# Decode logits of a hybrid decoder step: products on GpSimd, sums on VectorE

## The chip, the core and the metric

The kernel runs on one core of a Trainium2 chip. The metric is the device time of one execution in microseconds. Engines are named as in the profile: PE is TensorE, DVE is VectorE, ACT is ScalarE, POOL is GpSimd, SP is SyncE.

## What is computed

One step of a decoder with two parallel branches (attention and a gated short convolution), for a prompt of 512 rows plus 16 learned ones, and for 8 decode sequences of 4 new rows each with 512 past rows in a paged cache. All is float32; the model width is 2048, with 8 heads of 128 channels. Cut to what matters here:

```python
q, k, v, ga, cb, cc, ch, gc, ma, mc = split(rmsnorm(x) @ w_in)
z = einsum('bqhd,bkhd->bhqk', q, k) * HEAD_DIM ** -0.5 + b_sb      # the logits
log_keep = where(mask, log_sigmoid(-z), 0)
after = cumsum(log_keep, axis=3, reverse=True) - log_keep
attn = where(mask, exp(log_sigmoid(z) + after), 0)
a = einsum('bhqk,bkhd->bqhd', attn, v) * silu(ga)
c = cb * causal_conv(cc * ch) * silu(gc)
y = x + rmsnorm((sigmoid(ma + b) * (a @ w_pa) + sigmoid(mc + b2) * (c @ w_pc)) @ w_out)
```

The change concerns the logits `z` of the decode rows against their past: for each of the 8 sequences, 4 pages of 128 past keys, 8 heads and 4 query rows, a product over 128 channels.

## The kernel before

**Matrix products.** Weights are loaded by SP's queue in blocks of 1024 x 128 (`w_load`, L234, five buffers `raw`). `w_split` takes each apart: ACT casts the high part `whi` (L240), DVE subtracts it and writes the low part `wlo` (L241), in three buffers each. PE then makes three products per block and half of the rows (L256 plain, L944 in the scheme of seven products that the gate and output projections use, whose sums of weights DVE forms in L956 to L972). So every block that PE multiplies has first passed ACT and then DVE.

**Order of the stages.** First the norm of the rows and the first queries (to about 120 us); then the heads: `head_now` for four heads, with projections of k, v and q and the prompt's attention, whose masks POOL makes (L625), and `head_later` for four more; then the projections `pair` of the attention's gate, the convolution and the merge gates; then the rest of the attention, the two branch projections and the output.

**Decode attention** is a generator, `decode_steps`, which the other stages call for a step at a time (`dec_step`, `dec_group`), so that its instructions are written among theirs. A unit is a half of the heads and one sequence: 16 units of 4 pages. The first six units (`DEC1`) are called for by the heads, the other ten by the gate projections, one or two pages for each group of them. A unit loads its four query rows, broadcast to all 128 partitions, in two tiles `qb` of two rows and 4 heads x 128 channels (L745, POOL's queue, three buffers). Each page loads 128 keys, one to a partition, with 512 channels of four heads (`kpage`, L730, POOL's queue, three buffers). Then DVE works out 16 logits a key, each with one instruction (L754) that multiplies 128 channels of a key with those of a query, writes the products to a tile that nobody reads, and puts the sum into one column of `z_all`. After all pages the steps "logits", "weights" and "values" follow.

The order of the instructions within each engine is not the program's: a planner simulates the program on a timeline and writes each engine's order by it, except where `pin` (`keep_in_program_order`) ties an instruction to its place. `first` ties the loads of the first unit of each part. Once written, each engine's order is fixed and it works it off in order; semaphores hold an instruction until what it needs is done.

Of the kernel before, what the change touches and what calls it, by code (L numbers as in the profile page):

```python
# [9 lines left out]
F32 = mybir.dt.float32  # L10
# [3 lines left out]
ALU = mybir.AluOpType  # L14
# [3 lines left out]
P = 128  # L18
# [42 lines left out]
def hybrid_step_kernel(  # L61
# [7 lines left out]
    pe, act, dve, pool = nc.tensor, nc.scalar, nc.vector, nc.gpsimd  # L69
# [416 lines left out]
    z_all = dp.tile([P, NPG, DB, H, DT], F32, name="z_all")  # L486
# [239 lines left out]
    def page_load(t, cache, b, pg, cs):  # L726
        i = b * NPG + pg
        if i not in page_reg:
            page_reg[i] = pool.value_load(pt_i[0:1, i:i + 1], min_val=0, max_val=NPOOL - 1)
        return pool.dma_start(t, cache[bass.ds(page_reg[i], 1), :, cs].rearrange("o s c -> (o s) c"))  # L730

    def decode_steps():
# [2 lines left out]
        units = [(hf, b) for hf in range(2) for b in range(DB)]  # L735
        for said, part in (("part", units[:DEC1]), ("logits", units[DEC1:])):
            with tc.tile_pool(name="dec1", bufs=2, side="right") as d1:
                for hf, b in part:
                    cs = slice(hf * 512, (hf + 1) * 512)
                    qts = []  # L740
                    first = pin if (hf, b) in (units[0], units[DEC1]) else lambda x: x
                    for i in range(2):
                        qt = d1.tile([P, 2, 512], F32, name="qb", bufs=3)
                        r0 = b * DT + 2 * i
                        first(pool.dma_start(qt, q_scr[r0:r0 + 2, cs].unsqueeze(0).broadcast_to([P, 2, 512])))  # L745
                        qts.append(qt)
                    for pg in range(NPG):
                        kt = d1.tile([P, 512], F32, name="kpage", bufs=3)
                        first(page_load(kt, kc, b, pg, cs))
                        for i, qt in enumerate(qts):  # L750
                            for t in range(2):
                                for h in range(4):
                                    junk = d1.tile([P, P], F32, name="junk", bufs=2)
                                    dve.tensor_tensor_reduce(  # L754
                                        out=junk, in0=kt[:, h * P:(h + 1) * P], in1=qt[:, t, h * P:(h + 1) * P],
                                        scale=1.0, scalar=0.0, op0=ALU.mult, op1=ALU.add,
                                        accum_out=z_all[:, pg, b, 4 * hf + h, 2 * i + t:2 * i + t + 1])
                        yield
            yield said
        hl.append(hlctx.enter_context(tc.tile_pool(name="headin", bufs=1, side="right")))  # L760
        BHT = DB * H * DT
# [16 lines left out]
        with tc.tile_pool(name="dec2", bufs=1, side="right") as d2:  # L778
            def tl(name, n=1):
                return d2.tile([P, n * BHT], F32, name=name)  # L780

            e, l, r, t = tl("de", 4), tl("dl", 4), tl("dr", 4), tl("dt", 4)
# [39 lines left out]
        for g in range(2):  # L822
            for hf in range(2):
# [29 lines left out]
                for hh in range(4):  # L853
                    h = 4 * hf + hh
# [4 lines left out]
                yield  # L859

    dec = decode_steps()
    dec_at = set()

# [573 lines left out]
```

## Time and profile before

| | us |
|---|---|
| median of 3 runs | 1598.49 |
| lowest and highest | 1595.0 and 1600.42 |
| the profiled execution | 1598.94 |
| its span, first to last instruction | 1597.3 |
| granted TensorE clock in it | 0.993 of full speed |

The span is what the views of the trace cut up; times in them count from its start. A group's row reads: line, engine, operation, what it writes and reads, shapes, count, then the busy time, the mean nanoseconds of one, and the idle time of the engine just before them with what ended it. A row of a stretch reads: start and end, length, then for each engine the busy time and the number of its instructions, the granted clock, the share of DMA time and GB/s. A row of the timeline reads: start, duration, engine, line, operation, operands, count. The costliest groups by engine: PE's matmuls of L944 and L256, and on DVE the weight parts of L241 and the logits:

```profile
L241 DVE TENSOR_TENSOR wlo<-raw,whi 128x1024 fp32r<-128x1024 f32 x247 | 301.2, 1221 | 82.9 <-ACT whi L240 81.5
L754 DVE CUSTOM_DVE_ANT_0 junk<-kpage,qb 128x128 f32<-128x128 f32 x1024 | 245.1, 285 | 3.7 <-DMA qb<-q_scr 3.3
```

Consecutive instructions of DVE overlap in the records by some tens of nanoseconds, so a group's busy time can be more than it adds to the queue.

### The profile page before, as it was taken

The numbers are of one execution on the slowest core, as the hardware profiler recorded it, in microseconds if no ns is written. First come the engines' busy times: TensorE is split into PE (matmuls) and PEld (weight loads), VectorE is DVE, ScalarE is ACT, GpSimd is POOL, SyncE is SP. The second block draws the span as 40 slices with busy tenths as digits, with TensorE's granted clock in tenths as the row PEclk, the third lists the DMA queues.
The fourth block names the chain that finished last, engine by engine and source line by source line (L and its number), as shares of the span: only waits on it lengthen the run. The fifth ranks groups of instructions, "written<-read, shape, count | busy, mean of one in ns | idle before, by whom it ended". The sixth has DMA issues, their size and how long they took to land.

```text
span 1597.3 us, 32319 instructions
## 1 busy us (share of the span) xinstructions
PE 1567.6 (98%) x12172; PEld 1533.7 (96%) x12172; DVE 1268.8 (79%) x3574; ACT 752.7 (47%) x1339; POOL 234.6 (15%) x428
## 2 busy tenths in 40 slices
PE   9999999999999999999999999999899999999997
PEld 8999999999999999999999999999897789999997
DVE  6328999956799999999999996667666657877776
ACT  6335555435444444444454444446645543355562
POOL 1033333222111011010011100001203320000000
PEclk9999999999999999999999999999999999999999
DMA  8246556344555445355356554433868875433345
GB/s 247 81 137 180 169 164 187 110 127 138 167 162 146 139 140 150 117 152 159 107 180 187 161 155 130 125 121 115 279 186 265 253 240 179 152 101 99 100 137 187
DMA packets 300674, 252.77 MB, mean 158 GB/s; under 512 B 11521, under 2 KB 268613, under 8 KB 299701
## 3 DMA queue, kind: packets, MB, share of 16 engines
q1 hardware_dynamic: 272021, 160.45, 34.7%
q0 software_dynamic: 28368, 89.98, 17.0%
q8 instruction: 95, 1.56, 0.4%
q14 instruction: 62, 0.51, 0.1%
q10 hardware_dynamic: 128, 0.27, 0.1%
HBM read 217.95 MB, written 32.71 MB: 157 GB/s over the span
## 4 chain that ended last, share of the span: by engine, by line
PE 89%; DMA 4%; issue 2%; DVE 2%; ACT 1%; POOL 0%; DVEq 0%; POOLq 0%; SPq 0%; ACTq 0%
PE mm L944 32%; PE mm L256 24%; PE o L944 23%; DMA vpage<-in_cache_v 2%; PE mm L321 2%; PE z L321 1%; PE z L677 1%; PE o L687 1%; DMA raw<-in_w_in 1%; PE z L608 1%; PE z L1378 1%; DMA sg<-a_scr 1%; DMA gt<-gate_scr 1%; DVE wlo L241 1%; PE tp L829 0%
## 5 line engine op out<-in xcount | busy, mean ns | idle before, releaser
L240 ACT CAST whi<-raw 128x1024 fp32r<-128x1024 f32 x247 | 259.4, 1051 | 356.0 <-PE mm L944 122.3
L241 DVE TENSOR_TENSOR wlo<-raw,whi 128x1024 fp32r<-128x1024 f32 x247 | 301.2, 1221 | 82.9 <-ACT whi L240 81.5
L944 PE MATMUL mm<-h_hi,whi 128*128 128x272 f32 (+1 forms) x1152 | 332.6, 289 | 0.0
L944 PE MATMUL mm<-h_lo,whi 128*128 128x272 f32 (+1 forms) x1152 | 332.4, 289 | 0.0
L944 PE MATMUL mm<-h_hi,wlo 128*128 128x272 f32 (+1 forms) x1152 | 332.3, 290 | 0.0
L944 PE MATMUL o<-t_hi,whi 128*128 128x272 f32 (+1 forms) x864 | 250.0, 289 | 1.0 <-DVE c L970 1.0
L944 PE MATMUL o<-t_lo,whi 128*128 128x272 f32 (+1 forms) x864 | 250.2, 290 | 0.0
L944 PE MATMUL o<-t_hi,wlo 128*128 128x272 f32 (+1 forms) x864 | 249.8, 289 | 0.0
L754 DVE CUSTOM_DVE_ANT_0 junk<-kpage,qb 128x128 f32<-128x128 f32 x1024 | 245.1, 285 | 3.7 <-DMA qb<-q_scr 3.3
L944 PEld LDWEIGHTS mm<-h_hi,whi 128*128 128x128 f32 x1152 | 217.4, 189 | 0.0
L944 PEld LDWEIGHTS mm<-h_hi,wlo 128*128 128x128 f32 x1152 | 216.9, 189 | 0.1
L944 PEld LDWEIGHTS mm<-h_lo,whi 128*128 128x128 f32 x1152 | 216.8, 188 | 0.1
L241 DVE TENSOR_TENSOR wlo<-s,whi 128x1024 fp32r<-128x1024 f32 x126 | 154.0, 1222 | 63.9 <-ACT whi L240 62.5
L240 ACT CAST whi<-s 128x1024 fp32r<-128x1024 f32 x126 | 132.0, 1048 | 152.9 <-PE mm L944 52.8
L256 PE MATMUL mm<-h_lo,whi 128*128 128x280 f32 (+1 forms) x640 | 187.7, 293 | 0.0
L256 PE MATMUL mm<-h_hi,wlo 128*128 128x280 f32 (+1 forms) x640 | 187.1, 293 | 0.0
L256 PE MATMUL mm<-h_hi,whi 128*128 128x280 f32 (+1 forms) x640 | 186.7, 292 | 0.0
L944 PEld LDWEIGHTS o<-t_hi,whi 128*128 128x128 f32 x864 | 162.9, 189 | 1.5 <-DVE c L970 1.5
L944 PEld LDWEIGHTS o<-t_lo,whi 128*128 128x128 f32 x864 | 163.4, 189 | 0.5 <-issue 0.4
L944 PEld LDWEIGHTS o<-t_hi,wlo 128*128 128x128 f32 x864 | 163.1, 189 | 0.1
L256 PEld LDWEIGHTS mm<-h_lo,whi 128*128 128x128 f32 x640 | 120.4, 188 | 0.8
L256 PEld LDWEIGHTS mm<-h_hi,whi 128*128 128x128 f32 x640 | 120.5, 188 | 0.5
(390 smaller groups left out, 3181.1 us busy)
## 6 DMA issues: line engine op xcount, KB each, us to landing
raw<-in_w_in SPq DMA_DIRECT2D x192, 512.0 KB, 4.3
kpage<-in_cache_k POOLq DMA_DIRECT2D x64, 256.0 KB, 3.5
qb<-q_scr POOLq DMA_DIRECT2D x32, 512.0 KB, 5.7
vpage<-in_cache_v POOLq DMA_DIRECT2D x64, 256.0 KB, 5.8
raw<-in_w_out SPq DMA_DIRECT2D x32, 512.0 KB, 4.1
gate_scr<-g POOLq DMA_DIRECT2D x32, 272.0 KB, 4.6
gt<-gate_scr POOLq DMA_DIRECT2D x16, 544.0 KB, 3.9
raw<-in_w_pc SPq DMA_DIRECT2D x16, 512.0 KB, 4.4
```

What stands on the lines that cost most here:

```text
L240: act.copy(hi, x)
L241: dve.tensor_sub(lo, x, hi.bitcast(F32))
L256: pe.matmul(o, lhsT=w, rhs=r[:, t0:t1], start=(k == 0 and n == 0), stop=(k == nk - 1 and n == 2))
L321: pin(pe.matmul(o, lhsT=l, rhs=r[:, k, t0:t1], start=(start and m == 0), stop=(stop and m == 2), skip_group_check=True))
L608: pe.matmul(zt[:m, c0:c0 + n], lhsT=l[:, s0:s0 + m], rhs=r[:, ts:ts + n], start=(c0 == 0 and i == 0), stop=(i == 2), skip_group_check=True)
L677: pe.matmul(o, lhsT=l, rhs=x, start=False, stop=(i == len(ops) - 1), skip_group_check=True)
L687: pe.matmul(ot[:, ts - NMETA:ts - NMETA + n], lhsT=l[:m, st, :], rhs=x[:m, c0:c0 + n], start=False, stop=(g == GROUPS[-1] and i == 2), ski ...
L754: dve.tensor_tensor_reduce(out=junk, in0=kt[:, h * P:(h + 1) * P], in1=qt[:, t, h * P:(h + 1) * P], scale=1.0, scalar=0.0, op0=ALU.mult, o ...
L944: pe.matmul(o, lhsT=l[:, k, :], rhs=r, start=(start and k == 0 and m == 0), stop=(stop and k == 7 and m == 2), skip_group_check=True)
L1378: pin(pe.matmul(o, lhsT=(m1, m2)[h][:, k + 8 * (q == 1), ts], rhs=two[h][q == 2][:, :, k, :], start=(n == 0), stop=(n == 47)))
```

## The change

A page's 16 logits are no longer made by 16 instructions of DVE. For each of the two query tiles, POOL multiplies the page's 4 x 128 channels with the two query rows: one instruction writes 2 x 4 x 128 = 1024 products into a tile `kq` (two buffers). DVE then sums these over the 128 channels, one instruction for eight logits, and writes them to their eight places in `z_all`. Per page that is two multiplies on POOL and two sums on DVE; over the 64 pages 128 of each. The work on a page is also put one step later: a page's load is written, and then the products of the page before; the last page of each part follows at its end. The tile `junk` goes.

```diff
+                pages = []
+
+                def logits(qts, kt, hf, b, pg):
+                    for i, qt in enumerate(qts):
+                        kq = d1.tile([P, 2, 4, P], F32, name="kq", bufs=2)
+                        first(pool.tensor_mul(kq, qt.rearrange("p t (h d) -> p t h d", d=P),
+                                              kt.rearrange("p (h d) -> p h d", d=P).unsqueeze(1)
+                                              .broadcast_to([P, 2, 4, P])))
+                        first(dve.reduce_sum(
+                            z_all[:, pg, b, 4 * hf:4 * hf + 4, 2 * i:2 * i + 2].rearrange("p h t -> p t h"),
+                            kq, axis=mybir.AxisListType.X))
+
...
                         kt = d1.tile([P, 512], F32, name="kpage", bufs=3)
                         first(page_load(kt, kc, b, pg, cs))
-                        for i, qt in enumerate(qts):
-                            for t in range(2):
-                                for h in range(4):
-                                    junk = d1.tile([P, P], F32, name="junk", bufs=2)
-                                    dve.tensor_tensor_reduce(
-                                        out=junk, in0=kt[:, h * P:(h + 1) * P], in1=qt[:, t, h * P:(h + 1) * P],
-                                        scale=1.0, scalar=0.0, op0=ALU.mult, op1=ALU.add,
-                                        accum_out=z_all[:, pg, b, 4 * hf + h, 2 * i + t:2 * i + t + 1])
+                        pages.append((qts, kt, hf, b, pg))
+                        if len(pages) > 1:
+                            logits(*pages.pop(0))
                         yield
+                while pages:
+                    logits(*pages.pop(0))
             yield said
```

## The prediction

> **What bounds the kernel now.** I read the page first, then the busy time of each engine by stretch, then the waits of PE, the groups of DVE and POOL, and the timeline where DVE and POOL meet.
>
> ```profile
> span 1597.3 us, 32319 instructions
> ...
> PE 1567.6 (98%) x12172; PEld 1533.7 (96%) x12172; DVE 1268.8 (79%) x3574; ACT 752.7 (47%) x1339; POOL 234.6 (15%) x428
> ```
>
> PE is the bound: busy 1567.6 us of a span of 1597.3, so about 30 us at most are idle.
>
> ```profile
> L754 DVE DVE_READ_ACCUMULATOR2_ANT z_all<- x1024: 70/80/94, 125.7 to 946.4; 128x1 f32 x171
> ```
>
> The logits are written from 125.7 to 946.4 us, which I cut into stretches: six decode units beside the heads, a gap without logits, and the other ten units beside the gate projections.
>
> ```profile
> core 0: us, PE busy (x) PEld busy (x) DVE busy (x) ACT busy (x) POOL busy (x), PEclk, DMA share, GB/s
> 125.00:295.00 170.00, 170.00 (x1294) 165.18 (x1294) 164.01 (x916) 88.03 (x173) 54.37 (x106) 1.00 0.54 164
> 295.00:365.00 70.00, 70.00 (x548) 69.03 (x547) 47.60 (x72) 26.81 (x55) 17.25 (x30) 1.00 0.41 121
> 425.00:947.00 522.00, 520.96 (x4123) 520.32 (x4123) 501.59 (x1694) 232.42 (x344) 54.81 (x96) 1.00 0.50 149
> 947.00:1100.00 153.00, 153.00 (x1218) 153.00 (x1218) 104.24 (x101) 74.80 (x108) 7.79 (x15) 1.00 0.44 133
> ```
>
> ```profile
> PE o L944 <- DVE c L970: 1.0, 2, 0.6
> ```
>
> That last row is all that the list of PE's waits names between 80 and 1100 us: 1.0 us in two waits. Two things are to be seen. PE idles 522 - 520.96 = 1.04 us in the long stretch and not at all in the others: however much lighter DVE becomes, there is next to nothing to win. And DVE is busy 501.6 of 522 us and 164 of 170: it just keeps up. Whatever makes DVE's stream longer than the stretch makes PE wait for its weights, since L241 on DVE produces `wlo` for every block that PE multiplies, and DVE runs in order.
>
> **What goes from DVE.** Each of the 1024 logit instructions of L754 multiplies and sums 128 channels.
>
> ```profile
> 125.00:295.00 170.00, 92.17 (x768) 1.00 0.54 164
> 425.00:947.00 522.00, 153.06 (x1254) 1.00 0.50 149
> ```
> ```profile
> 240.14 0.28 DVE L754 CUSTOM_DVE_ANT_0 junk<-kpage,qb 128x128 f32<-128x128 f32 x1
> 240.35 0.28 DVE L754 CUSTOM_DVE_ANT_0 junk<-kpage,qb 128x128 f32<-128x128 f32 x1
> ...
> 240.86 0.72 DVE L754 CUSTOM_DVE_ANT_0 junk<-kpage,qb 128x128 f32<-128x128 f32 x1
> 241.51 0.08 DVE L754 DVE_READ_ACCUMULATOR2_ANT z_all<- 128x1 f32 x1
> ```
>
> These are L754's rows in the two stretches (half of the count are reads of the accumulator, which overlap the next instruction) and a piece of DVE's timeline. Starts lie 0.21 us apart, which is what one costs its queue. So 384 x 0.21 = 81 us leave the first stretch, and 627 x 0.21 = 132 us the second. DVE keeps 164 - 81 = 83 us and 501.6 - 132 = 370 us of other work.
>
> **What comes to DVE.** 24 pages with two sums each in the first stretch (48), and 627 / 16 = 39 pages (78) in the second; each sums 1024 numbers into eight.
>
> ```profile
> 502.42 1.22 DVE L241 TENSOR_TENSOR wlo<-s,whi 128x1024 fp32r<-128x1024 f32 x1
> 503.56 0.28 DVE L754 CUSTOM_DVE_ANT_0 junk<-kpage,qb 128x128 f32<-128x128 f32 x1
> ```
>
> No sum of this size is in the trace; the nearest row passes 1024 elements and frees the queue after 503.56 - 502.42 = 1.14 us. I take 1.14: 55 us and 89 us. Were that all, DVE would be busy 138 of 170 us and 459 of 522, lighter than now, and the time would not move.
>
> **What comes to POOL.** As many multiplies, 1024 products from two SBUF operands each.
>
> ```profile
> L150 POOL TENSOR_SCALAR_AFFINE_SELECT tri<-tri 128x128 f32<-128x128 f32 x1 | 0.3, 292 | 0.0
> L135 POOL TENSOR_TENSOR rtmp<-rtmp 128x1 f32<-128x1 f32 x1 | 0.2, 193 | 0.1
> L773 POOL TENSOR_SCALAR_AFFINE_SELECT z_new<-z_new 32x256 f32<-32x256 f32 x1 | 0.9, 919 | 0.3 <-ACT z_new L813 0.3
> ```
>
> An operation on one element takes 193 ns, a flat one of 128 takes 292: (292 - 193) / 127 = 0.78 ns an element for one input. Two inputs, if they are read one after the other, make 1.56 ns, so 0.19 + 1.6 = 1.8 us; that is the lower end. The select over four-dimensional patterns costs (919 - 193) / 255 = 2.85 ns an element, so 3.1 us; the upper end. The multiply's patterns are long runs of 128, which is nearer to the flat select; I take 2.3. That is 48 x 2.3 = 110 us and 78 x 2.3 = 179 us. The Trainium skill (GPSIMD Engine Reference, section Performance versus the Vector engine) measures 4497 ns for 2048 elements, half of which is an estimate of 2.25 us, and no run here shows it.
>
> POOL has room by itself: 54.8 + 179 us in 522, 54 + 110 in 170. The question is whether it may work while DVE does.
>
> **Do the two run side by side?** These are POOL's small instructions near 30 us, DVE's at that time, and POOL's masks beside the last L754 quoted above.
>
> ```profile
> 30.14 0.19 POOL L135 TENSOR_TENSOR rtmp<-rtmp 48x1 f32<-48x1 f32 x1
> 30.40 1.25 POOL L136 TENSOR_TENSOR rtmp<-rtmp 48x1 f32<-48x1 f32 x1
> ```
> ```profile
> 30.38 1.23 DVE L315 TENSOR_TENSOR wlo<-raw,whi 128x1024 fp32r<-128x1024 f32 x1 [0.37 <-ACT whi L310]
> ```
> ```profile
> 240.88 0.55 POOL L625 TENSOR_SCALAR_AFFINE_SELECT e<-e 128x128 f32<-128x128 f32 x2
> 241.37 0.35 POOL L625 TENSOR_SCALAR_AFFINE_SELECT eA<-eA 128x112 f32<-128x112 f32 x1
> ```
>
> A POOL product of one element takes 0.19 us at 30.14; the next starts 20 ns behind a 1.23 us DVE instruction with two SBUF inputs, takes 1.25 us, and ends with it (31.65 against 31.61). The other way round, an L754 takes 0.72 us instead of 0.28 at 240.86, while POOL runs its masks. Neither slows the other a little: each waits the other out. The Trainium skill (SBUF — State Buffer, section Who interferes with whom) says the same: a DVE instruction with two SBUF inputs and a GpSimd instruction that reads SBUF lock each other out for a whole instruction, while a reduction never contends. The trace agrees in the rows above; no run here has a reduction beside POOL. By this rule the change does not take products off a busy port. It puts slower ones on it.
>
> So in each stretch the times of DVE's two-input work and of POOL's multiplies add up. What may lie beside a multiply are the new sums, and DVE's operations that read one operand from PSUM.
>
> ```profile
> L975 DVE TENSOR_TENSOR c<-mm,s 128x272 f32<-128x272 f32 (+1 forms) x25 | 10.9, 437 | 1.5 <-PE mm L944 0.7
> L970 DVE TENSOR_TENSOR c<-o,s 128x272 f32<-128x272 f32 (+1 forms) x25 | 10.9, 435 | 0.0
> ```
>
> In the second stretch that is 89 + 22 = 111 us of sums and PSUM readers, in the first the 55 us of sums. How much of it meets a multiply depends on the order that the planner writes; the bounds are none and all. I take half, because a multiply that is released by a sum starts when DVE has already gone on to a two-input instruction, but the second sum of a page can lie beside it.
>
> - Second stretch: 370 + 89 + 179 - 55 = 583 us of work in 522: 61 us late.
> - First stretch: 83 + 55 + 110 - 27 = 221 in 170: 51 us late. Behind it, from 295 to 365, DVE is idle 70 - 47.6 = 22 us, which gives back 22: 29 us late.
>
> The sum is 90 us. The span and what lies around it make 1598.94 in the profiled execution, 0.03% above the median of the runs, so I leave that difference out: 1598.9 + 90 = 1689 us. Ends: with 1.8 us and everything beside the multiplies, 370 + 89 + 140 - 111 = 488 of 522 and 83 + 55 + 86 - 55 = 169 of 170, no loss; with 3.1 us and nothing beside them, 370 + 89 + 242 = 701 (179 late) and 83 + 55 + 149 = 287 (117 - 22 = 95 late), 274 us. With half beside, 1.8 gives 22 + 5 = 27 us and 3.1 gives 124 + 68 = 192 us.
>
> **Waits and queues.**
>
> ```profile
> kpage<-in_cache_k POOLq DMA_DIRECT2D x64, 256.0 KB, 3.5
> qb<-q_scr POOLq DMA_DIRECT2D x32, 512.0 KB, 5.7
> ```
> ```profile
> L625 POOL TENSOR_SCALAR_AFFINE_SELECT r<-r x16: 243/339/1174, 130.5 to 275.3; 128x128 f32<-128x128 f32 x12, 16x16 f32<-16x16 f32 x4
> L625 POOL TENSOR_SCALAR_AFFINE_SELECT e<-e x16: 239/304/434, 147.0 to 286.6; 128x128 f32<-128x128 f32 x12, 16x16 f32<-16x16 f32 x4
> ```
>
> These are two DMA issues with their time to landing, and POOL's masks of the heads. The new wait is DVE's sum on POOL's multiply. Behind a waiting sum stand the `wlo` of L241 and, in the heads, the softplus and split steps, for which ACT and then PE wait. The multiply waits for a page loaded one page earlier; it lands 3.5 us after its issue, and a page's work is spread over 522 / 39 = 13 us or 170 / 24 = 7 us, so that wait costs nothing. In POOL's queue the page loads, the masks of L625 and the stores of the gates and heads now stand behind up to two multiplies, 4.6 us. Only the masks are in a chain that PE needs, and they cost POOL's turn rather than more work; I leave them inside the range. With three `qb` buffers and the last page still unread, the second query load of a unit waits for that page's first multiply; the unit's first page is itself one step behind, which covers its 5.7 us.
>
> **Rivals.**
>
> *No contention worth the name.* If the multiplies land mostly beside sums, PSUM readers and DVE's idle time, DVE needs 459 us of 522 and PE remains the bound: 1598.9 - 1.0 = 1598 us, not slower. For it speaks the low end above, and that the planner leaves the placing of 126 multiplies free. Against it: of the 459 us only 111 can lie beside a multiply, and 179 are asked for. It decides where price and overlap bring the sum of the second stretch under 522: 1.8 us with two thirds beside.
>
> *Faster.* Relief of DVE speeds up the weights: bounded by PE's idle 1.04 us, and by matmuls that come later than their best pitch.
>
> ```profile
> 500.00:600.00 100.00, 100.00 (x794) 99.90 (x793) 97.61 (x307) 45.20 (x74) 11.41 (x20) 1.00 0.50 145
> 700.00:800.00 100.00, 99.39 (x787) 99.12 (x786) 95.79 (x308) 41.01 (x61) 8.80 (x16) 1.00 0.46 134
> 1000.00:1100.00 100.00, 100.00 (x797) 100.00 (x796) 67.25 (x64) 50.28 (x73) 5.41 (x10) 1.00 0.41 124
> ```
>
> Where DVE is 67% busy PE starts 797 matmuls in 100 us, beside the logits 794 and 787. Even ten lost in every 100 us of the 522, at 100 / 797 = 0.125 us each, are 52 x 0.125 = 7 us, the most that there is: 1592 us, and only if the new order is better everywhere.
>
> *POOL's queue alone.* No lock, but masks behind multiplies: 32 masks of L625 in the rows above, each up to 2.3 us late and a quarter of that reaching PE (the quarter is a guess), 18 us: 1617 us. For it, the masks stand between DVE's softplus and ACT's splits; against it, PE has projections in between.
>
> **How the numbers follow.** Forecast (lock, DVE late) 0.73; POOL's queue alone 0.06; no contention 0.13; faster 0.08. About 0.3% (5 us) is what a measurement can tell from no change. Slower takes 0.79, same 0.13, faster 0.08. The forecast's own range is 1626 to 1791 at half overlap. For 8 in 10 I reach down to 1594, which takes in no effect and half of the faster case, and cut the top at 1760, where price and overlap would both have to be bad.
>
> **What would show it.** Right: in the long stretch DVE's L241, 1.22 us now, has a longer mean, POOL's multiplies vary with DVE's work from about 2.3 us upwards, and PE's list of waits names DVE `wlo` (or ACT behind it) with tens of microseconds between 125 and 947; after 950 nothing changes. Wrong: multiplies of constant length, `wlo` at 1.22 us, DVE near 88% in the long stretch, and PE without waits. A multiply well under 1.8 us, or DVE's instructions unchanged in length beside one, would undo the sum.

## The result, and the profile after

The changed kernel takes 1801.72 us (median of 4 runs, 1797.96 to 1805.91); the kernel before took 1598.02 beside it. The ratio is 1.127, with a 95% interval of 1.125 to 1.130. It is slower, as forecast, but by 204 us instead of 90, and outside the range. The profiled execution has a span of 1796.4 us, 199.1 more than before. Ratios here and below leave out slow executions, of which there was one: 3572 us, among the four of e2.

From the page of the changed kernel: its span, the engines' busy time, and the groups that answer to L241 and L754 of before.

```profile
span 1796.4 us, 30466 instructions
...
PE 1643.0 (91%) x12172; PEld 1588.3 (88%) x12172; DVE 1405.6 (78%) x1654; ACT 752.5 (42%) x1339; POOL 596.1 (33%) x556
...
L241 DVE TENSOR_TENSOR wlo<-raw,whi 128x1024 fp32r<-128x1024 f32 x247 | 378.1, 1532 | 113.0 <-ACT whi L240 111.6
L743 POOL TENSOR_TENSOR kq<-qb,kpage 128x1024 f32<-128x1024 f32 x128 | 365.5, 2863 | 142.4 <-DVE z_all L746 132.0
...
L746 DVE TENSOR_REDUCE z_all<-kq 128x8 f32<-128x1024 f32 x128 | 153.6, 1206 | 2.3 <-POOL kq L743 2.3
```

DVE has 1920 instructions fewer and yet is busy 1405.6 - 1268.8 = 137 us longer. The `wlo` of L241 did not change, but its mean went from 1221 to 1532 ns. PE's busy time grew by 75 us with the same 12172 matmuls, and its idle time from 30 to 153 us. These are the longest of its waits:

```profile
PE o L953 <- DVE c L979: 28.8, 9, 5.1
PE mm L953 <- DVE wlo L241: 23.5, 17, 4.8
PE o L953 <- ACT whi L240: 17.1, 10, 4.9
PE o L953 <- DVE wlo L241: 15.3, 12, 2.3
PE mm L953 <- ACT whi L240: 11.9, 16, 4.2
```

A row reads: what waited for what, total us, times, longest us. So DVE's `wlo` is in it with 38.8 us, as the prediction's sign had it, beside L979, where DVE reads PE's accumulator `o`. The next rows are the answer on the tile `kq` (shortest, median and longest in nanoseconds, first and last start), then a piece of DVE's timeline in the second part of the logits, and POOL's at the same time.

```profile
L743 POOL TENSOR_TENSOR kq<-qb,kpage x128: 2339/2767/4446, 123.3 to 869.5; 128x1024 f32<-128x1024 f32 x128
L746 DVE TENSOR_REDUCE z_all<-kq x128: 1151/1207/1223, 130.8 to 873.4; 128x8 f32<-128x1024 f32 x128
```
```profile
644.64 1.21 DVE L241 TENSOR_TENSOR wlo<-s,whi 128x1024 fp32r<-128x1024 f32 x1
...
649.12 3.38 DVE L965 TENSOR_TENSOR s<-raw 128x1024 f32<-128x1024 f32 x1
652.43 0.43 DVE L979 TENSOR_TENSOR c<-o,s 128x272 f32<-128x272 f32 x1
652.78 1.20 DVE L746 TENSOR_REDUCE z_all<-kq 128x8 f32<-128x1024 f32 x1
653.90 1.21 DVE L241 TENSOR_TENSOR wlo<-raw,whi 128x1024 fp32r<-128x1024 f32 x1
655.03 3.38 DVE L976 TENSOR_TENSOR raw<-raw 128x1024 f32<-128x1024 f32 x1
```
```profile
644.82 6.60 POOL L743 TENSOR_TENSOR kq<-qb,kpage 128x1024 f32<-128x1024 f32 x2 [2.57 <-DVE z_all L746]
651.72 0.58 POOL L730 DMA_DIRECT2D kpage<-in_cache_k  x1 [0.30 <-POOL kq L743]
654.07 3.26 POOL L743 TENSOR_TENSOR kq<-qb,kpage 128x1024 f32<-128x1024 f32 x1 [1.78 <-DVE z_all L746]
```

The lock is as the prediction had it. At 654.07 a multiply starts while the L241 of 653.90 runs; it takes 3.26 us instead of 2.34 and ends at 657.33. L976, issued at 655.03, takes 3.38 us instead of 1.22. The sums never lengthen: 1.15 to 1.22 us in all 128.

Where the time goes is seen best when the n-th matmul of PE is compared in both traces (both have 12172). This table is worked out from the start times: the time of the kernel before at that matmul, and then the microseconds by which each other kernel stands behind it. The kernels e1 to e10 are those of the next section.

```
matmul  before  after     e1     e2     e3     e4     e5     e6     e7     e8     e9    e10
  1050   148.3    3.7    3.3   -3.5    2.9   -2.7   -3.9   -1.5   -2.6   -1.2   -2.2   -2.5
  2550   344.5   26.9   26.7   -3.5   28.1    0.3    1.0   18.3   18.8    3.3   -2.2   -2.4
  3050   407.7   54.2   53.2   -3.5   49.5    0.3    1.0   65.8   18.8    3.3   14.2   -2.4
  4050   534.7  112.3   53.5   56.7   70.6   37.1    3.4   84.2   51.6   56.3   15.4   -1.5
  5300   692.8  204.5   53.4  152.6   91.2   60.8    3.4  104.1  110.2   96.1   15.4   -1.5
  8300  1071.7  203.4   53.7  151.5  151.3   59.7    4.2  157.2  115.3   95.0   14.3   -2.6
 11800  1539.6  199.0   47.9  148.7  151.9   57.4    0.9  156.6  111.1   90.0   -0.0    1.9
```

The changed kernel loses 27 us in the first part of the logits, 27 more just behind it, 150 in the second part, and nothing afterwards. The rows by stretch, in the columns of the prediction: the second part, the piece just behind the first part, a stretch after both, and the first part.

```profile
477.00:875.00 398.00, 305.09 (x1986) 290.08 (x1984) 396.99 (x301) 107.30 (x162) 276.43 (x149) 0.87 0.38 115
```
```profile
394.00:442.00 48.00, 30.54 (x167) 28.00 (x166) 47.05 (x65) 21.26 (x32) 3.91 (x7) 0.75 0.20 57
```
```profile
1000.00:1150.00 150.00, 150.00 (x1194) 150.00 (x1194) 100.81 (x93) 71.64 (x100) 8.11 (x15) 1.00 0.42 127
```
```profile
131.00:393.00 262.00, 245.89 (x1782) 236.45 (x1781) 215.73 (x210) 102.24 (x206) 189.58 (x180) 0.95 0.45 134
```

DVE is full in the first two rows and PE starves. But the second part has shrunk: its sums run from 477 to 875 us, and in that time PE does only the 1986 matmuls that took it 252 us before (from 423 to 674). The prediction spread the same pages over 522. Behind it, from 1000 us on, DVE idles a third of the time, as it did before. The first part is another case: DVE is busy only 216 of 262 us, and PE still does there in 262 us what took it 232 before. Of these 30 us, 16 are idle time of PE, mostly behind the split steps of the heads on DVE (L495); the other 14 are matmuls that took longer, at a granted clock of 0.95.

### The profile page after: what moved, and what is told of

Its sections match the earlier page's. It is cut to its first block, busy times and chain, and to the rows that moved or that the text cites. A ratio compares the mean times of both kernels' runs of the same rounds, so it can differ in the third digit from the quotient of the medians.

```text
span 1796.4 us, 30466 instructions
## 1 busy us (share of the span) xinstructions
PE 1643.0 (91%) x12172; PEld 1588.3 (88%) x12172; DVE 1405.6 (78%) x1654; ACT 752.5 (42%) x1339; POOL 596.1 (33%) x556
## 4 chain that ended last, share of the span: by engine, by line
PE 65%; DVE 24%; issue 6%; DMA 2%; ACT 2%; POOL 0%; DVEq 0%; SPq 0%; ACTq 0%
PE mm L953 21%; PE mm L256 19%; PE o L953 17%; DVE wlo L241 7%; DVE z_all L746 4%; PE mm L321 2%; DVE raw L976 1%; DVE s L968 1%; PE z L677 1%; DVE s L965 1%; PE z L321 1%; DMA sg<-a_scr 1%; PE o L687 1%; DMA raw<-in_w_in 1%; DVE s L981 1%
## 5 line engine op out<-in xcount | busy, mean ns | idle before, releaser
L241 DVE TENSOR_TENSOR wlo<-raw,whi 128x1024 fp32r<-128x1024 f32 x247 | 378.1, 1532 | 113.0 <-ACT whi L240 111.6
L743 POOL TENSOR_TENSOR kq<-qb,kpage 128x1024 f32<-128x1024 f32 x128 | 365.5, 2863 | 142.4 <-DVE z_all L746 132.0
L953 PE MATMUL o<-t_hi,whi 128*128 128x272 f32 (+1 forms) x864 | 268.0, 310 | 51.6 <-DVE c L979 28.8
L953 PE MATMUL o<-t_hi,wlo 128*128 128x272 f32 (+1 forms) x864 | 266.9, 309 | 15.3 <-DVE wlo L241 15.3
L241 DVE TENSOR_TENSOR wlo<-s,whi 128x1024 fp32r<-128x1024 f32 x126 | 177.5, 1409 | 88.7 <-ACT whi L240 88.3
L953 PEld LDWEIGHTS mm<-h_hi,wlo 128*128 128x128 f32 x1152 | 222.1, 193 | 27.6 <-DVE wlo L241 27.5
L953 PEld LDWEIGHTS mm<-h_hi,whi 128*128 128x128 f32 x1152 | 222.9, 194 | 16.6 <-ACT whi L240 15.6
L953 PEld LDWEIGHTS o<-t_hi,whi 128*128 128x128 f32 x864 | 178.9, 207 | 56.7 <-DVE c L979 31.1
L953 PEld LDWEIGHTS mm<-h_lo,whi 128*128 128x128 f32 x1152 | 222.1, 193 | 4.9 <-DVE h_lo L916 4.9
L746 DVE TENSOR_REDUCE z_all<-kq 128x8 f32<-128x1024 f32 x128 | 153.6, 1206 | 2.3 <-POOL kq L743 2.3
L256 PEld LDWEIGHTS mm<-h_hi,wlo 128*128 128x128 f32 x640 | 124.3, 194 | 1.6 <-DVE wlo L241 0.8
```

The lines of the kernel that those rows point to most:

```text
L241: dve.tensor_sub(lo, x, hi.bitcast(F32))
L256: pe.matmul(o, lhsT=w, rhs=r[:, t0:t1], start=(k == 0 and n == 0), stop=(k == nk - 1 and n == 2))
L743: first(pool.tensor_mul(kq, qt.rearrange("p t (h d) -> p t h d", d=P), kt.rearrange("p (h d) -> p h d", d=P).unsqueeze(1) .broadcast_to([P ...
L746: first(dve.reduce_sum(z_all[:, pg, b, 4 * hf:4 * hf + 4, 2 * i:2 * i + 2].rearrange("p h t -> p t h"), kq, axis=mybir.AxisListType.X))
L953: pe.matmul(o, lhsT=l[:, k, :], rhs=r, start=(start and k == 0 and m == 0), stop=(stop and k == 7 and m == 2), skip_group_check=True)
```

## The experiments

The theory after the result has three parts. DVE and POOL lock each other out, so sums of busy time are right. The planner puts the pages into too short a stretch of PE's work, where DVE is overfull (packing, below). And the DVE work between the two parts, which waits for the first part to end, comes too late. Rivals were a fixed loss per page wherever it stands, and the waits between POOL and DVE by themselves.

| kernel | median us | ratio to before (95%) |
|---|---|---|
| e1, first six units alone | 1647.24 | 1.031 (1.029 to 1.034) |
| e2, last ten units alone | 1748.94 | 1.095 (1.091 to 1.098) |
| e3, last ten spread | 1751.80 | 1.098 (1.095 to 1.102) |
| e4, POOL only writes | 1655.34 | 1.035 (1.032 to 1.039) |
| e5, spread, POOL only writes | 1602.45 | 1.004 (1.003 to 1.006) |
| e6, spread, multiplies in quarters | 1758.11 | 1.102 (1.098 to 1.106) |
| e7, multiplies on DVE | 1708.47 | 1.070 (1.068 to 1.071) |
| e8, half of the products | 1687.14 | 1.056 (1.054 to 1.058) |
| e9, before with a late first part | 1600.35 | 1.001 (0.999 to 1.002) |
| e10, before with lighter products | 1598.62 | 1.000 (0.998 to 1.002) |

**e1 and e2: one part alone.** In each, the other part keeps the old instructions; the diff is e1's, and e2 asks for "logits" instead of "part".

```diff
-                        pages.append((qts, kt, hf, b, pg))
+                        if said == "part":
+                            pages.append((qts, kt, hf, b, pg))
...
+                        else:
+                            for i, qt in enumerate(qts):
...
+                                        dve.tensor_tensor_reduce(
...
```

> Only the six units beside the heads take the new form, the other ten keep the old instructions. Packing theory (the loss arises where the planner puts the pages, and can be read off from how late PE is at the same matmul: 54 us at matmul 3050 of the changed kernel, 27 of it at the sums for the gate projections that wait for the first part's room): about 1598 + 54 = 1652 us, and those sums again start only behind the last sum of the first part. Rival, loss per page (the multiplies cost what they cost wherever they stand, 199 us for 64 pages): 199 x 24 / 64 = 75, so 1673 us. If the first part costs nothing by itself: 1598.

> Only the ten units beside the gate projections take the new form. Packing theory: the 40 pages again lie beside some 285 us of PE's work instead of 522, DVE is saturated there, and PE is 150 us late at their end: about 1748 us. Rival, loss per page: 199 x 40 / 64 = 124, so 1722 us. The two runs together should make 54 + 150 = 204 by the first theory, 199 by the second.

Measured 1647 and 1749: the first theory said 1652 and 1748, the rival 1673 and 1722. The table of matmuls shows e1 losing 53 us up to matmul 3050 and nothing after it, e2 nothing up to there and 152 after it. The two parts are independent, and a page of the second costs more (152 / 40 = 3.8 us) than one of the first (53 / 24 = 2.2 us).

The end of the first part can be read in DVE's timeline: of the kernel before, of the changed kernel, and of e9, where the first part was made longer.

```profile
293.98 0.08 DVE L754 DVE_READ_ACCUMULATOR2_ANT z_all<- 128x1 f32 x1
294.10 1.37 DVE L916 TENSOR_TENSOR r<-h_hi 128x548 f32<-128x548 f32 x2
```
```profile
391.32 1.20 DVE L746 TENSOR_REDUCE z_all<-kq 128x8 f32<-128x1024 f32 x1
392.55 2.65 DVE L925 TENSOR_TENSOR r<-h_hi 128x548 f32<-128x548 f32 x4
```
```profile
352.61 0.07 DVE L754 DVE_READ_ACCUMULATOR2_ANT z_all<- 128x1 f32 x1
352.71 2.01 DVE L916 TENSOR_TENSOR r<-h_hi 128x548 f32<-128x548 f32 x3
```

L916 (L925 after the change) is the first of the sums that the gate projections need in their scheme of seven products. In all three it follows the last logit of the first part at once; by the code, these sums are written into the room that this part's tiles leave. Below, this place between the two parts is called the seam. Before, DVE did them from 294 on while PE still had heads to multiply. After the change they begin at 392, when PE is already at the product that reads them: the row from 394 to 442 above has PE busy 30.5 of 48 us.

**e9: the late seam in the kernel before.** The old instructions, and `DEC1 = 9` instead of 6.

> The kernel before, with its old instructions, but nine units in the first part instead of six, and seven in the second: no POOL work, no lock. The first part's pages then end later (36 pages at 170 / 24 = 7 us from 125 on: about 380 instead of 294). If the sums for the gate projections (28 instructions of DVE and their splits) start only when the first part has ended, and PE has by then reached the product that needs them, they start at about 380 and PE idles there some 20 to 30 us: 1615 to 1628. Rival, the sums do not wait for the first part, or the planner fills the gap: 1596.

The sums of the seam did follow the longer first part, at 352.7, and PE lost 17.6 us there (from -2.2 to 15.4 in the table). But the whole is 1600 us, not 1615 to 1628: the delay was given back behind 1137 us, where PE waits 10.1 us for DVE's L1153 in the kernel before and only 2.7 us in e9. So the mechanism is shown, and its price in the total is not: the changed kernel, which keeps 9.4 us of that wait (L1162), gave back only 4 us in the same place. Why e9 loses the wait and the changed kernel does not is open.

**e3: the second part spread out.** Page loads and multiplies of the last ten units are tied to POOL's program order; a unit's last page is done ahead of the next unit's loads, so that three `qb` buffers suffice.

```diff
+                    while pages and said == "logits":
+                        logits(*pages.pop(0))
-                    first = pin if (hf, b) in (units[0], units[DEC1]) else lambda x: x
+                    first = pin if said == "logits" or (hf, b) == units[0] else lambda x: x
...
-                        first(dve.reduce_sum(
+                        dve.reduce_sum(
```

> All units in the new form, but page loads and multiplies of the last ten are tied to the program's order on POOL, so that they come one or two for each group of the gate projections, over some 640 us of PE's work. Packing theory: the first part stays 54 us late, the second costs 370 x 640 / 522 + 91 + 187 - 55 = 677 against 640 at the most, so 0 to 61 us: 1652 to 1713 us. Rival, loss per page: no change, 1798 us.

A miss for both. The pages did spread, over 659 us of PE's work, and the second part costs 103 us instead of 150; the theory allowed 61. Its waits of PE, the stretch of its second part, and a piece of DVE's and PE's timelines:

```profile
PE o L955 <- DVE c L981: 55.0, 17, 6.6
```
```profile
473.00:1235.00 762.00, 687.24 (x5211) 677.60 (x5211) 695.12 (x598) 297.16 (x434) 297.87 (x188) 0.96 0.42 125
```
```profile
626.26 3.31 DVE L967 TENSOR_TENSOR s<-raw 128x1024 f32<-128x1024 f32 x1
629.50 1.21 DVE L746 TENSOR_REDUCE z_all<-kq 128x8 f32<-128x1024 f32 x1
630.62 1.21 DVE L978 TENSOR_TENSOR raw<-raw 128x1024 f32<-128x1024 f32 x1
631.76 3.36 DVE L241 TENSOR_TENSOR wlo<-raw,whi 128x1024 fp32r<-128x1024 f32 x1
635.04 1.21 DVE L746 TENSOR_REDUCE z_all<-kq 128x8 f32<-128x1024 f32 x1
636.17 0.43 DVE L981 TENSOR_TENSOR c<-o,s 128x274 f32<-128x274 f32 x1
```
```profile
636.65 0.60 PE L955 MATMUL o<-t_hi,whi 128*128 128x274 f32 x1 [6.56 <-DVE c L981]
```

DVE is busy only 695 of 762 us, and still PE idles 75 us, 55 of them behind L981. (The other 28 of the 103 us are matmuls that took longer, at a granted clock of 0.96.) L981 reads PE's accumulator `o`, which PE's next product must wait for; its turn on DVE comes at 636.17, behind a page's two sums and an L241 that a multiply held for 3.36 us. PE has been idle 6.56 us when it starts again. So DVE need not be full to make PE late: a page puts a burst into the middle of a chain with little slack. A sum of busy times against the length of a stretch is then a lower bound, not the loss.

**e4 and e5: POOL writes but does not read.** Two clears of `kq` (0.96 us each) stand where a multiply stood, in the program of the changed kernel (e4) and in that of e3 (e5). The products are left out. Not only the reading goes: two clears take 1.93 us where a multiply took 2.34 at the least, and they no longer wait for the loads of pages and queries, so the planner's order is not quite the same either.

```diff
-                        first(pool.tensor_mul(kq, ...))
+                        for n in range(2):
+                            first(pool.memset(kq, 0.0))
```

> POOL reads nothing: in the place of each multiply it clears the tile twice, so the products are left out and the sums are of zeros; queue, waits, buffers and DVE's sums stay. Lock on reading: DVE's two-input instructions keep 1.22 us and the time falls to about 1600 us, with POOL still busy beside DVE. Rival, the waits (sum on POOL, POOL on buffer) and the order are the cost: stays near 1790. Rival, any work of POOL locks DVE: DVE's instructions are as long as in the changed kernel and the time stays over 1700.

> The spread order of the third run with the clears of the fourth: POOL reads nothing (products left out, sums of zeros), and the pages of the last ten units follow the program's order on POOL. If the loss is made of the planner's packing (60 us in the fourth run, where nothing but the sums was packed) and of the lock (the rest), both are gone here: 1596 to 1612 us. Rival, the waits between POOL and DVE or the order on POOL cost by themselves: over 1650.

In e4 these are POOL's clears and the two groups of L241:

```profile
L744 POOL MEMSET kq<- 128x1024 f32 x256 | 243.4, 964 | 115.6 <-DVE z_all L745 107.2 <-DVE r L651 3.4
```
```profile
L241 DVE TENSOR_TENSOR wlo<-raw,whi 128x1024 fp32r<-128x1024 f32 x247 | 300.9, 1221 | 124.8 <-ACT whi L240 121.5 <-ACT e L681 2.1
L241 DVE TENSOR_TENSOR wlo<-s,whi 128x1024 fp32r<-128x1024 f32 x126 | 154.0, 1223 | 99.0 <-ACT whi L240 98.7
```

POOL is busy 243 us with its clears, and L241 is back at 1221 ns. Taken one by one from the records, the 82 instructions of L241 that run beside a clear have a mean of 1217 ns; in the changed kernel, the 91 beside a multiply have 2325 and the other 282 have 1221. It is POOL's reading that holds DVE. That answers to the rule of the Trainium skill weighed in the prediction (SBUF — State Buffer, section Who interferes with whom), which sets a GpSimd instruction that only writes apart from one that reads. The first part loses nothing any more. The second still loses 60 us in e4, more than expected; in e5, with its pages spread, that is gone too, and 1602 us fall into the expected 1596 to 1612. The waits between POOL and DVE and the order on POOL, as far as e5 keeps them, thus cost next to nothing (0.4%); read lock and packing together make the loss. How e4's 60 us came about is seen in three rows of its second part:

```profile
449.00:530.00 81.00, 68.87 (x510) 68.03 (x510) 56.63 (x63) 27.24 (x40) 42.07 (x55) 0.94 0.69 217
530.00:610.00 80.00, 70.36 (x510) 67.52 (x508) 78.27 (x87) 28.67 (x46) 54.73 (x62) 0.96 0.29 85
610.00:722.00 112.00, 101.84 (x738) 98.90 (x737) 109.65 (x127) 40.12 (x62) 66.74 (x73) 0.94 0.35 100
```

At 530 us PE is 26 us late. Until then DVE has been idle a third of the time, and L964 has waited 24 us for `raw` loads, while 25 of the part's 40 page loads were issued; that these held the weights up is likely, not shown. The other 35 us are lost behind 530, where DVE is full with sums.

**e6: shorter holds.** e3 with each multiply cut into four of 256 products.

```diff
-                        first(pool.tensor_mul(kq, ...))
+                        for t in range(2):
+                            for h in (0, 2):
+                                first(pool.tensor_mul(kq[:, t, h:h + 2].rearrange("p h d -> p (h d)"),
+                                                      qt[:, t, h * P:(h + 2) * P], kt[:, h * P:(h + 2) * P]))
```

> The spread order of the third run (1752 us), each multiply cut into four of 256 products. Together they cost POOL more (4 x about 0.73 = 2.9 us for 2.34), but each holds DVE for a shorter time. If what is left there (about 105 us beside the last ten units, with DVE only 91% busy) comes from the length of a single hold, which PE's few ready weights do not cover: clearly below, 1690 to 1725. Rival, the sum of the holds decides: the same or slower, 1752 to 1800.

1758 against 1752 us: the number is the rival's. The pieces take 0.71 us at least, 2.85 for the four. The second part's loss falls by a tenth only (from 103 to 94 us), and the first part's grows. The length of a single hold is not what matters most. Nor is DVE's busy time: over the second part it falls from 695 to 655 us, and the loss hardly does. PE's wait for the read of `o` fell from 55.0 to 25.6 us, that for `wlo` in the same products rose from 18.9 to 39.4. What sets the loss of the spread kernels is thus known only in part.

**e7: no multiplies on POOL.** DVE multiplies and sums, with the same two instructions.

```diff
-                        first(pool.tensor_mul(kq, ...))
+                        first(dve.tensor_mul(kq, ...))
```

> The multiplies of the changed kernel on DVE instead of POOL: 2 x 1.14 us a query tile for 8 x 0.21 = 1.68 before, 77 us more on DVE in all, and no POOL. The planner knows what DVE's instructions cost, so no stretch should be overfilled: 83 + 48 x 2.28 = 192 against 170 + 22 idle behind it, and 370 + 182 = 552, which may spread to 1000 us: 1598 to 1630. Rival, a longer DVE stream costs its whole length because PE has no slack: 1675.

It took 1708 us, beyond both numbers. The stretch of the second part:

```profile
442.00:825.00 383.00, 325.98 (x2258) 312.69 (x2257) 381.98 (x418) 123.98 (x189) 43.32 (x74) 0.92 0.44 130
```

DVE is busy 382 of 383 us, with no lock anywhere. In this time PE does what took it 287 us before (423 to 710). DVE's other work in that piece is 208 us in the trace of before; with 80 x 1.14 for the sums and as much for the multiplies that is 390, and 390 - 287 = 103 us too much. PE loses 96. So the planner overfills the stretch even where neither engine holds the other, and the theory's statement that it would not was wrong. A longer DVE stream, packed so, costs 96 us without any lock.

**e8: half of the products.** Each multiply makes one query row, and the sum adds it for both, so half of the logits are copies of the others.

```diff
-                        first(pool.tensor_mul(kq, ...))
+                        first(pool.tensor_mul(kq[:, 0], qt[:, 0]..., kt...))
...
-                            kq, axis=mybir.AxisListType.X))
+                            kq[:, 0:1].broadcast_to([P, 2, 4, P]), axis=mybir.AxisListType.X))
```

> The changed kernel with half of the products: each multiply makes the 512 of one query row, and the sums add those twice, so half of the logits are wrong copies. Sums, waits, queue and packing stay, the lock's time halves (128 x about 1.27 us). If the last ten units lose 60 us by packing and 90 by the lock: 60 + 45 = 105, and the first six 54 / 2 = 27: 1730 us. Rival, the lock's length does not matter, only the number of multiplies: 1798.

```profile
L743 POOL TENSOR_TENSOR kq<-qb,kpage x128: 1257/1372/3807, 122.4 to 684.8; 128x512 f32<-128x512 f32 x128
```

1687 us instead of 1730: the first part loses 3 us, not 27, since POOL keeps up and the seam stays at 292. The second loses 93 (105 expected), in 177 us of PE's work: with multiplies at half the price the planner packs closer still.

**e10: relief alone.** The kernel before, each logit over the first 64 of its 128 channels.

```diff
-                                        out=junk, in0=kt[:, h * P:(h + 1) * P], in1=qt[:, t, h * P:(h + 1) * P],
+                                        out=junk[:, :64], in0=kt[:, h * P:h * P + 64], in1=qt[:, t, h * P:h * P + 64],
```

> The kernel before with each logit taken over the first 64 of the 128 channels (half of every product and sum left out): DVE's 1024 instructions cost about 0.14 us instead of 0.21, some 70 us less DVE work, nothing added anywhere. If DVE is no bound before the change: 1590 to 1598, no difference over 0.3%. Rival, DVE at 95% beside the logits does slow PE: below 1590.

```profile
PE 1565.4 (98%) x12172; PEld 1531.2 (96%) x12172; DVE 1206.7 (75%) x3574; ACT 750.9 (47%) x1339; POOL 236.2 (15%) x428
```

DVE's busy time falls by 62 us and the time stays, 1.000 (0.998 to 1.002). The change had nothing to win, even without its costs, and none of the versions tried beats the kernel before.

## Why the prediction was right in direction and wrong in size

- **No gain to be had**: right. PE was idle 1.04 us in the long stretch, and relief alone (e10) moves nothing.
- **The prices**: right. A multiply takes 2.34 us at the least (taken 2.3), a sum 1.21, with the next start 1.13 us later (taken 1.14).
- **The lock**: right. The prediction's sums raise DVE's busy time by 583 - 501.6 = 81 and 221 - 164 = 57 us, 138 in all; measured 137. e4 shows the cause: without the reading, L241 is at 1.22 us.
- **Half of the free work beside the multiplies**: too much. By the records it is 13 of 58 us in the first part and 46 of 113 in the second, 59 us in all where the prediction took 82. Multiplies also ran for 24 us while DVE was idle, which the prediction had not counted; that the two make up the 82, and the total fits, is luck.
- **"61 us late" in the second stretch**: this is the step that failed, and 89 of the missing 114 us are here. It set 583 us of work against 522. The pages came to lie beside 252 us of PE's work. With the prediction's own prices there: 181 us of other DVE work in that piece, 80 x 1.14 = 91, 80 x 2.34 = 187, less half of the free work there (91 + 10), 51, make 408, and 408 - 252 = 156 us late. Measured 146 across that piece, 150 with its edges. So the mechanism was right, and the length that the work was set against was wrong. I had taken over the placing of the old kernel, although the text said that the planner is free; that was named as something that could only help.
- **"Behind it ... gives back 22"** in the first stretch: failed. 51 us late was too much for the stretch itself (27 at matmul 2550), since the pages ran on to 392 us; and it was not a full DVE that cost the 27, as the sum of 221 in 170 had it, but waits for the heads' split steps, which the prediction named and gave no price, and slower matmuls. Nothing came back: the idle time of DVE from 295 to 365 was the cover of the sums at the seam, which wait for the first part, and they cost 27 more. The prediction forecast 29 for the part, and e1 has 48 to 53.
- **The range** ended at 1760 because I held bad price and bad overlap together to be unlikely. The price was as taken, and the total on DVE too; a third quantity, the stretch, was not among the bounds.
- **POOL's queue alone** and **no contention**: both fell, e5 for the first and L241's mean for the second.
- **After 950 us nothing changes**: right in substance; from matmul 5300 on the delay stays between 199 and 204.5 us.

What stays open: why the planner takes the shorter stretch to have room (it does so with DVE's own instructions too, e7), how much the lower granted clock adds in the first part and in the spread kernels (below), and why the delay at the seam was given back in e9 and hardly in the changed kernel.

## What to carry to other kernels

Before work is moved to POOL, add its reading time to the two-input work of DVE in the stretch where both will run: here about 215 us of products left DVE, and its busy time grew by 137 us. Then ask in which stretch the planner will put it, because a stretch of half the length turned 61 us into 150; the placing of the old instructions says little about the new. And look for what waits behind the end of the moved work: idle time of an engine can be the cover of a step that must not come late.

## What the runs showed of the hardware that was not expected

- The granted clock is lower where PE starves. Over the second part of the changed kernel it is 0.87 on average, in the row from 477 to 875 above, and at the seam 0.75; the same 1986 matmuls are busy 305 us in the second part against 252 us before. DVE is busy 396.99 of the 398 us there and 47.05 of 48 at the seam, so faster matmuls could have won some 2 us at most in the two. In the first part (0.95) and in e3 and e6 (0.96 in the second part) DVE is not full, and whether the slower matmuls cost time of their own there, the runs do not separate.
- Sums beside multiplies keep their length in every run (1151 to 1223 ns in the changed kernel, where 44 of the 128 lie beside one), which agrees with what the prediction drew from the Trainium skill (SBUF — State Buffer, section Who interferes with whom) on reductions.
- A clear on POOL leaves a two-input DVE instruction alone but not every one-input one. These are DVE's scalings in e4 and in the kernel before:

```profile
L1051 DVE TENSOR_SCALAR cv<-u,wcv x16: 293/544/1257, 528.7 to 817.5; 128x512 f32<-128x512 f32 x8, 128x32 f32<-128x32 f32 x8
```
```profile
L1043 DVE TENSOR_SCALAR cv<-u,wcv x16: 293/506/546, 500.9 to 757.9; 128x512 f32<-128x512 f32 x8, 128x32 f32<-128x32 f32 x8
```

The longest goes from 0.55 to 1.26 us beside clears (two of them, at 529.15 and 634.45 us), while the `wlo` next to them stay at 1.22.
